# Three gates over the mixers' end, and the mixers' masks and operand products on VectorE, in a one-core hybrid encoder block

## The chip, the cores and the metric

The kernel runs on one core of a Trainium2 chip. The metric is the device time of one execution in microseconds, as the median of three runs. One execution more was taken with the hardware profiler; the profile and the trace are of that execution.

## The reference

One layer of a trunk (256 tokens, width 2048, float32). Every product of a weight matrix with the activations is done in the kernel as a few products of parts (a rounded high part and a low rest), so nearly all of its time is TensorE work on weight tiles.

```python
def hybrid_mixer(u, w_in, ...):
    proj = u @ w_in
    sb, fox, rw, gates = _split(proj, (3 * SB_WIDTH, 3 * FOX_WIDTH + FOX_HEADS, RWKV_IN, N_BRANCHES * D_MODEL))
    y_a = _merge_heads(stick_breaking_attention(...))     # 4 heads x 128, masked strictly below the diagonal
    y_b = _merge_heads(forgetting_attention(...))         # 4 heads x 128
    y_c = rwkv7_time_mix(rw, ...)                         # 16 heads x 64, a recurrence over the 256 tokens
    g_a, g_b, g_c = _split(jax.nn.sigmoid(gates), (D_MODEL,) * 3)
    m = g_a * (y_a @ w_branch_a) + g_b * (y_b @ w_branch_b) + g_c * (y_c @ w_branch_c)
    return m @ w_out

def reference(x, ...):
    u = _rms_norm(x, norm_mix_pre[l])
    x = x + _rms_norm(hybrid_mixer(u, ...), norm_mix_post[l])
    hdn = jnp.square(jax.nn.relu(_rms_norm(x, norm_mlp_pre[l]) @ w_mlp_up[l]))
    x = x + _rms_norm(hdn @ w_mlp_down[l], norm_mlp_post[l])
```

In the stick-breaking attention, `a = where(strict, exp(log_beta + between), 0)`, with the logs masked by the same strict triangle before they are summed.

## The kernel before

**The weight stream.** All weights lie in device memory as one sequence of tiles of 128 x 1024 numbers (512 KB each), `wst`. `wraw` (L159) has SyncE fetch the next tile into one of three `raw` buffers; `wpos` is the place in the sequence and the table `jump` (L153) says where the sequence is left for another place. `wsplit` (L169) makes of each tile a rounded part on ScalarE (L172, `whi`) and the rest on VectorE (L174, `wlo`); three buffers of each. TensorE then multiplies: `unit` (columns, L190, L194, L196) and `tok` (tokens, L234, and L219 for the last tile, which is kept for both token halves). A product on `wlo` has to wait for VectorE's subtraction of that tile, and a tile is prepared one ahead (`AHEAD`).

**The mixers.** The attention and recurrence are one generator, `mixers()`: `sb_mix`, `fox_mix`, `rwkv_lora`, then `rwkv_half` twice (heads 0 to 7 and 8 to 15). It yields between pieces of its work. `tick` (L137), called a few times in each weight tile, lets the generator go on: each tick adds credit, each yield takes off the number that it yields, and a yield of `("stage", cost, hold)` also stops the generator until `hold` worth of ticks have passed (2.0 if none is named). So the yielded numbers and holds set at which place of the weight stream each piece of the mixers stands.

**Order on the engines.** From the first stage on, TensorE's order is the order in which the code is written (a manual schedule of that engine); ScalarE, VectorE and GpSimd are ordered by a scheduler. Each engine then runs its instructions strictly in order.

**The pieces that the change touches.**
- `sb_mix`: the scores `z` (L503, L504 make two logs), masked by the strict triangle `mst` on the diagonal blocks of each head, 8 GpSimd products of 128 x 128 (L507); the masked logs are split (L513, L514) and summed on TensorE (L519 to L522); after the exponential (L534) the same mask again, 8 GpSimd products (L537), ahead of the products with the values (L542, L543).
- `rwkv_half`, `gates`: for each of its four head pairs the scan of log decays (L734), exponentials `ep` and `em` (L737, L738), and the operands of the chunk products: `At` on VectorE (L751, L753) and `Bt` on GpSimd, one product from the normalised key (L750), one from the receptance `r` (L758). TensorE multiplies `At` with `Bt` (L775); the result is masked on VectorE into `SC` (L784). The gates' small projections are L723 (TensorE).
- `rwkv_half`, the triangular inverse: 32 x 32 blocks are transposed into `U` (L814, VectorE), 31 steps of forward substitution (L819, L821) fill `Ti`, and then three more transposes write `TW` (L825) and the blocks of `SC` (L829, twice) that TensorE reads (L834).
- `rwkv_half`, the end: for each two head pairs a group norm (`rsqrt`, L264 to L269), scale, bias, the bonus `bon` and the output gate (L936 to L939), which gives `yc`. TensorE's last instructions of the mixers are L100, L101, L926 and L929.

**The mixers' end.** After the projections of the mixers the stream goes on with gates and branches: `gate` (a projection of `u`, 8 tiles, then a tanh on ScalarE, L1003) and `branch` (a product with the mixers' result, 4 tiles for the third branch). The third branch needs `yc`. So two of its four gates are run first (`thc`, L1033), in which the mixers go on by ticks; what is left of the mixers after that is issued at once (L1034, L1035). `cut` (L1025) splits each finished `yc` into a `pk` tile (L255 on ScalarE, L256 on VectorE). Then come branch 0, branch 1, gate 2, branch 2, gate 3 and branch 3 of the third branch; the evacuations are L1014 and L1015.

```python
    thc = [gate(), gate("BK", 8)]                        # L1033
    while not fin[0]:
        step()
    cut()
```

Names in the trace: `pk` operands are split activations (`u` or `yc`), `g` are the mixers' 128 x 256 tiles, `gn` the group norm's, `gps` are PSUM banks of the weight stream and `mps` those of the mixers.

## Time and profile before

| | us |
|---|---|
| median of 3 runs | 1519.75 |
| lowest, highest | 1519.08, 1521.86 |
| the profiled execution, its own time | 1519.93 |
| span of its trace, first to last instruction | 1518.2 |
| TensorE busy (share of the span) | 1495.3 (98%) |
| VectorE busy | 1208.3 (80%) |
| ScalarE busy | 939.7 (62%) |
| GpSimd busy | 99.6 (7%) |
| mean granted TensorE clock | 0.996 |

In the rows of the profile PE is TensorE's multiplication and PEld its loading of weights, DVE is VectorE, ACT ScalarE, POOL GpSimd, SP SyncE. A row of the timeline reads: start in us from the span's start, duration in us, engine, line, operation, what is written and read, shape, count, and in brackets the engine's idle time before it and what ended it. Successive instructions of one engine may overlap a little, so what an instruction adds to a queue is the distance from its start to the next one's. Equal instructions that follow each other are merged into one row. A few records of matmuls can be missing.

The stages of the span that matter here: `sb_mix` runs from about 65 to 130 us, the gates of the recurrence at 225 to 265 (first half) and 447 to 480 (second half), the two triangular inverses end at 332 and 553, the mixers' end is at 657.6. What follows (the output projection, then the MLP from 845 on) is the same code before and after.

### The profile page before, as it was taken

The numbers are of one execution on the slowest core, as the hardware profiler recorded it, in microseconds if no ns is written. First come the engines' busy times: TensorE is split into PE (matmuls) and PEld (weight loads), VectorE is DVE, ScalarE is ACT, GpSimd is POOL, SyncE is SP. The second block draws the span as 40 slices with busy tenths as digits, with TensorE's granted clock in tenths as the row PEclk, the third lists the DMA queues.
The fourth block names the chain that finished last, engine by engine and source line by source line (L and its number), as shares of the span: only waits on it lengthen the run. The fifth ranks groups of instructions, "written<-read, shape, count | busy, mean of one in ns | idle before, by whom it ended". The sixth has DMA issues, their size and how long they took to land.

```text
span 1518.2 us, 22692 instructions
## 1 busy us (share of the span) xinstructions
PE 1495.3 (98%) x8384; PEld 1254.8 (83%) x8384; DVE 1208.3 (80%) x1663; ACT 939.7 (62%) x1433; POOL 99.6 (7%) x151
## 2 busy tenths in 40 slices
PE   9999999999999999989999999999999999999997
PEld 7888888887787877778888988888888888888886
DVE  7875669985678885565656778999899989999996
ACT  7665677545776445644445766677666666766663
POOL 0031003000002000000000000000000000000000
PEclk9999999999999999999999999999999999999999
DMA  7645454454455464445575758879888888889874
GB/s 266 194 167 181 148 172 156 157 190 144 157 170 181 145 195 147 156 152 194 203 249 189 242 173 263 235 226 275 247 256 265 242 249 245 263 263 259 253 221 151
DMA packets 104687, 312.71 MB, mean 206 GB/s; under 512 B 10240, under 2 KB 12288, under 8 KB 104576
## 3 DMA queue, kind: packets, MB, share of 16 engines
q1 hardware_dynamic: 93968, 279.87, 55.2%
q0 software_dynamic: 8064, 29.36, 10.1%
q10 hardware_dynamic: 2544, 2.03, 0.5%
q8 instruction: 66, 1.08, 0.3%
q14 instruction: 45, 0.37, 0.1%
HBM read 279.77 MB, written 2.10 MB: 186 GB/s over the span
## 4 chain that ended last, share of the span: by engine, by line
PE 86%; DVE 6%; DMA 3%; issue 2%; ACT 2%; DVEq 0%; POOLq 0%; SPq 0%; POOL 0%; ACTq 0%
PE gps L234 25%; PE gps L190 19%; PE gps L194 11%; PE gps L219 7%; PE mps L1363 3%; PE mps L1365 3%; PE mps L1364 3%; PE gps L1363 2%; PE gps L1365 2%; PE gps L1364 2%; DMA raw<-in_wst_dram 2%; DVE wlo L174 2%; PE gps L196 1%; ACT whi L172 1%; DMA raw<-raw 1%
## 5 line engine op out<-in xcount | busy, mean ns | idle before, releaser
L174 DVE TENSOR_TENSOR wlo<-raw,whi 128x1024 fp32r<-128x1024 f32 x576 | 697.7, 1221 | 176.0 <-ACT whi L172 158.5
L172 ACT ACTIVATE whi<-raw 128x1024 fp32r<-128x1024 f32 x576 | 603.9, 1056 | 257.1 <-PE gps L234 91.7
L190 PE MATMUL gps<-pk,whi 128*128 128x512 f32 x1479 | 375.7, 392 | 1.8 <-DVE tmp L1281 1.6
L190 PEld LDWEIGHTS gps<-pk,whi 128*128 128x128 f32 x1479 | 273.9, 188 | 57.7 <-DVE tmp L1281 2.6
L234 PE MATMUL gps<-whi,pk 128*128 128x512 f32 x1004 | 254.6, 392 | 0.0
L194 PEld LDWEIGHTS gps<-pk,wlo 128*128 128x128 f32 x1582 | 215.5, 190 | 15.7 <-DVE wlo L174 0.8
L194 PE MATMUL gps<-pk,wlo 128*128 128x256 f32 x1582 | 221.1, 282 | 0.0
L234 PEld LDWEIGHTS gps<-whi,pk 128*128 128x128 f32 x1004 | 186.4, 188 | 39.7 <-issue 0.8
L234 PE MATMUL gps<-wlo,pk 128*128 128x512 f32 x502 | 137.7, 392 | 1.1 <-DVE wlo L174 1.1
L234 PEld LDWEIGHTS gps<-wlo,pk 128*128 128x128 f32 x502 | 93.2, 188 | 21.9 <-DVE wlo L174 2.0
L1363 PE MATMUL mps<-whi,fm 128*128 128x512 f32 x224 | 88.6, 396 | 0.8 <-ACT whi L172 0.5
L1364 PE MATMUL mps<-whi,fm 128*128 128x512 f32 x224 | 87.7, 392 | 0.0
L1280 ACT ACTIVATE tmp<-gps 128x256 f32<-128x256 f32 x64 | 24.6, 384 | 101.7 <-PE gps L196 99.8
L1365 PE MATMUL mps<-wlo,fm 128*128 128x512 f32 x224 | 87.4, 390 | 0.0
L1343 POOL DMA_DIRECT2D raw<-raw x56 | 48.8, 872 | 573.2 <-DVE raw L1340 279.8
L1340 DVE TENSOR_TENSOR raw<-raw,raw 128x1024 f32<-128x1024 f32 x56 | 68.3, 1220 | 0.8
L219 PE MATMUL gps<-whi,pk 128*128 128x512 f32 x224 | 63.0, 404 | 4.6 <-ACT pk L255 4.6
L1363 PE MATMUL gps<-whi,fm 128*128 128x512 f32 x168 | 65.8, 392 | 0.0
L1365 PE MATMUL gps<-wlo,fm 128*128 128x512 f32 x168 | 65.8, 392 | 0.0
L1364 PE MATMUL gps<-whi,fm 128*128 128x512 f32 x168 | 65.5, 390 | 0.0
L219 PEld LDWEIGHTS gps<-whi,pk 128*128 128x128 f32 x224 | 42.3, 193 | 14.4 <-ACT pk L255 5.0
L1365 PEld LDWEIGHTS mps<-wlo,fm 128*128 128x128 f32 x224 | 42.1, 188 | 9.6 <-DVE wlo L174 0.2
(346 smaller groups left out, 1732.2 us busy)
## 6 DMA issues: line engine op xcount, KB each, us to landing
raw<-in_wst_dram SPq DMA_DIRECT2D x516, 512.0 KB, 4.4
raw<-raw POOLq DMA_DIRECT2D x56, 512.0 KB, 8.2
x<-in_xt_dram SPq DMA_DIRECT2D x8, 256.0 KB, 6.8
x<-in_x_dram SPq DMA_DIRECT2D x8, 256.0 KB, 5.0
raw<-in_wst_dram SPq DMA_DIRECT2D x4, 256.0 KB, 4.8
g<-in_gains_dram SPq DMA_DIRECT2D x4, 256.0 KB, 4.9
pk<-in_gains_dram SPq DMA_DIRECT2D x4, 256.0 KB, 7.4
out_dram<-x SPq DMA_DIRECT2D x4, 256.0 KB, 2.8
```

The source lines that it names most:

```text
L172: A.activation(hi, raw, AF.Copy)
L174: low = lambda: V.tensor_tensor(lo, raw, hi.bitcast(F32), ALU.subtract)
L190: PE.matmul(ps, hi[:, i * 128:i * 128 + 128], pks[i], start=first and i == 0, stop=False)
L194: PE.matmul(ps[:, 0:T], lo[:, i * 128:i * 128 + 128], pks[i][:, 0:T], start=False, stop=False)
L219: PE.matmul(ps[tt], pks[k][:, c:c + 128], w[:, (k - k0) * 512:(k - k0) * 512 + 512], start=k == 0 and part == 0 and w is hl[0], stop=w is ...
L234: PE.matmul(ps[tt], pks[k][:, c:c + 128], w[:, (k - k0) * 512:(k - k0) * 512 + 512], start=k == 0 and part == 0 and w is hl[0], stop=False)
L1280: A.activation(b, ps[:, T:2 * T], AF.Copy)
L1340: V.tensor_tensor(R[d, a], R[d, a], R[d, b], ALU.add)
L1343: G.dma_start(out=R[d, a], in_=R[d, b], accum_op=ALU.add)
L1363: PE.matmul(Q[f], a, w, start=d == d0 and i == 0, stop=False)
L1364: PE.matmul(Q[f], b, w, start=False, stop=False)
L1365: PE.matmul(Q[f], a, wl, start=False, stop=d == dn and i == 1)
```

## The change

Four things are changed.

1. Three gates of the third branch run before its first branch product, not two, and the table `jump` takes the third gate's 8 weight tiles out of their place accordingly. The third gate's tanh lies in two tiles of the tag `BK`, as the second's does.
2. The strict masks of `sb_mix` are done on VectorE, two heads and both diagonal blocks in one instruction of 128 x 2 x 2 x 128 numbers: four VectorE products take the place of sixteen GpSimd ones. The yields there have other costs and shorter holds.
3. The two `Bt` products of each head pair are done on VectorE (16 in all).
4. In `rwkv_half` each transpose of 32 x 32 blocks is cut in two halves with a yield after each; the hold after a head pair's first chunk products is 3.5 for the first pair (it was 2.0), the holds around the last transposes are smaller.

```diff
-    jump = {23: 28, 53: 24, 27: 54, gc + 7: gc + 12, gc + 19: gc + 8, gc + 11: gc + 20}
+    jump = {23: 28, 53: 24, 27: 54, gc + 7: gc + 12, gc + 19: gc + 24, gc + 31: gc + 8,
+            gc + 11: gc + 20, gc + 23: gc + 32}
...
+    def masked(x):
+        d = x.rearrange("p h (b c) -> p h b c", b=3)[:, :, 0:3:2, :]
+        V.tensor_tensor(d, d, C("mst").unsqueeze(1).unsqueeze(1).to_broadcast([128, 2, 2, 128]), ALU.mult)
...
-            for h in (2 * hp, 2 * hp + 1):
-                for c in (0, 256):
-                    G.tensor_tensor(z[:, h, c:c + 128], z[:, h, c:c + 128], C("mst"), ALU.mult)
-            yield ("stage", 1.8, 2 + 6 * hp)
+            masked(z[:, hs])
+            yield ("stage", 2.3, 1)
...
-            for h in (2 * hp, 2 * hp + 1):
-                for c in (0, 256):
-                    G.tensor_tensor(m0[:, h, c:c + 128], m0[:, h, c:c + 128], C("mst"), ALU.mult)
-            yield ("stage", 0.2, 1 + 8 * hp)
+            masked(m0[:, hs])
+            yield ("stage", 0.9, 1 + 2 * hp)
...
-            G.tensor_tensor(Bt[p][:, :, 0:64], kn4, ep[:, :, 0:64], ALU.mult)
+            V.tensor_tensor(Bt[p][:, :, 0:64], kn4, ep[:, :, 0:64], ALU.mult)
...
-            G.tensor_tensor(Bt[p][:, :, 64:128], r.rearrange("p (c t) -> p c t", c=4), ep[:, :, 1:65], ALU.mult)
+            V.tensor_tensor(Bt[p][:, :, 64:128], r.rearrange("p (c t) -> p c t", c=4), ep[:, :, 1:65], ALU.mult)
...
-            yield ("stage", 1.6)
+            yield ("stage", 1.6, 3.5 if i == 0 else 2.0)
...
-            V.transpose(out=U[br], in_=SC[br, :, 32 * b:32 * b + 32].rearrange("s l t -> s t l"))
-            yield 1.3
+            for c in (slice(0, 16), slice(16, 32)):
+                V.transpose(out=U[br, c], in_=SC[br, :, 32 * b:32 * b + 32][:, :, c].rearrange("s l t -> s t l"))
+                yield 0.65
...
-        V.transpose(out=TW[0:32].rearrange("t l i -> t i l"), in_=Ti[0:32].rearrange("l t i -> l i t"))
-        yield 1.3
+        for c in (slice(0, 16), slice(16, 32)):
+            V.transpose(out=TW[0:32, :, c].rearrange("t l i -> t i l"), in_=Ti[0:32, :, c].rearrange("l t i -> l i t"))
+            yield 0.65
...
-            V.transpose(out=SC[br, :, 32 * b:32 * b + 32].rearrange("i l t -> i t l"), in_=Ti[br])
-            yield ("stage", 1.3, 1 + 3 * b)
+            for c in (slice(0, 16), slice(16, 32)):
+                V.transpose(out=SC[br, :, 32 * b:32 * b + 32][:, :, c].rearrange("i l t -> i t l"), in_=Ti[br, c])
+                yield ("stage", 0.65, 0.5 + 3 * b * (c.start > 0))
...
-    thc = [gate(), gate("BK", 8)]
+    thc = [gate(), gate("BK", 8), gate("BK", 8)]
```

Four lines are added on the whole, so a line of the kernel after stands one to four lines below its fellow before (L174 is L175, L219 is L220, L234 is L235, L255 is L256, L750 is L751, L929 is L933, L1003 is L1007).

**How the instructions move: TensorE at the mixers' end.** Before, after the mixers' last TensorE instructions, the stream goes on with the first tile of branch 0, whose activation operands (`pk_5947`, `pk_5950`) are split `yc`:

```order
L929 MATMUL mps_6517<-zz,gup_6480 128x256
L929 MATMUL mps_6518<-zz,gup_6480 128x256
L234 MATMUL gps_6546<-whi_6496,pk_5947 128x512 x2
L234 MATMUL gps_6547<-whi_6496,pk_5947 128x512 x2
L234 MATMUL gps_6546<-whi_6496,pk_5950 128x512 x2
L234 MATMUL gps_6547<-whi_6496,pk_5950 128x512 x2
L234 MATMUL gps_6546<-wlo_6497,pk_5947 128x512
```

Now the same two instructions stand in the second tile of the third gate, whose operands (`pk_267` to `pk_279`) are split `u`:

```order
L933 MATMUL mps_6553<-zz,gup_6500 128x256
L933 MATMUL mps_6554<-zz,gup_6500 128x256
L235 MATMUL gps_6514<-wlo_6519,pk_267 128x512
L235 MATMUL gps_6515<-wlo_6519,pk_267 128x512
L235 MATMUL gps_6514<-whi_6536,pk_268 128x512 x2
L235 MATMUL gps_6515<-whi_6536,pk_268 128x512 x2
L235 MATMUL gps_6514<-whi_6536,pk_269 128x512 x2
```

After these rows come the rest of that tile and six more gate tiles, and only then the four tiles of branch 0; before, branch 0 came at once. In both, the first three tiles of branch 0 read `yc` 0 to 5 and the last one (L219, now L220) reads `yc` 6 and 7.

**ScalarE at the same place.** Before, the splits of the last two `yc` (`pk_6540`, `pk_6543`) come behind the group norm's tables and three weight tiles, and the next gate's tanh is far behind them:

```order
L172 ACTIVATE whi_6568<-raw_6566 128x1024
L265 ACT_TABLE_LOAD
L265 ACTIVATE gn_6485<-gn_6485 128x512
L172 ACTIVATE whi_6586<-raw_6584 128x1024
L172 ACTIVATE whi_6604<-raw_6602 128x1024
L172 ACTIVATE whi_6628<-raw_6626 128x1024
L937 ACTIVATE g_1119_5867<-g_1119_5867,par 128x256
L937 ACTIVATE g_1120_5868<-g_1120_5868,par 128x256
L255 ACTIVATE pk_6540<-g_1119_5867 128x256
L255 ACTIVATE pk_6543<-g_1120_5868 128x256
```

Now they stand ahead of the third gate's tanh (`th_6684`, `th_6692`):

```order
L173 ACTIVATE whi_6620<-raw_6618 128x1024
L173 ACTIVATE whi_6638<-raw_6636 128x1024
L941 ACTIVATE g_1122_5887<-g_1122_5887,par 128x256
L941 ACTIVATE g_1123_5888<-g_1123_5888,par 128x256
L173 ACTIVATE whi_6656<-raw_6654 128x1024
L256 ACTIVATE pk_6588<-g_1122_5887 128x256
L256 ACTIVATE pk_6615<-g_1123_5888 128x256
L173 ACTIVATE whi_6674<-raw_6672 128x1024
L173 ACTIVATE whi_6698<-raw_6696 128x1024
L1007 ACTIVATE th_6684<-gps_6514 128x512
L1007 ACTIVATE th_6692<-gps_6515 128x512
```

What moved is the third gate's evacuation, from behind two branches to just behind the last split.

**VectorE in the gates of the first half.** The piece is where the second head pair's operands are made. Before (`wlo` rows are the weight tiles 73 and 74 of the kernel's whole ones):

```order
L174 TENSOR_TENSOR wlo_2405<-raw_2402,whi_2404 128x1024
L640 TENSOR_SCALAR g_449_2352<-tmp_2354,omu,zp_2355 128x256
L762 TENSOR_TENSOR hl_2376<-g_442_2319,hl_2376 128x256
L745 TENSOR_SCALAR kkr_2417<-g_331_1830,par,b_376_2045 128x256
L174 TENSOR_TENSOR wlo_2448<-raw_2445,whi_2447 128x1024
L743 TENSOR_TENSOR g_466_2414<-g_466_2414,g_331_1830 128x256
L746 TENSOR_SCALAR tha_2381<-tha_2381,em_2382 128x256
L753 TENSOR_TENSOR At_2420<-g_466_2414,em_2382 128x4x64
L751 TENSOR_SCALAR At_2420<-kkr_2417,tha_2381 128x4x64
```

Now, the same two tiles:

```order
L175 TENSOR_TENSOR wlo_2393<-raw_2390,whi_2392 128x1024
L763 TENSOR_TENSOR hl_2364<-g_442_2307,hl_2364 128x256
L746 TENSOR_SCALAR kkr_2405<-g_331_1818,par,b_376_2033 128x256
L744 TENSOR_TENSOR g_466_2402<-g_466_2402,g_331_1818 128x256
L747 TENSOR_SCALAR tha_2369<-tha_2369,em_2370 128x256
L751 TENSOR_TENSOR Bt_2409<-kkr_2405,ep_2371 128x4x64
L752 TENSOR_SCALAR At_2408<-kkr_2405,tha_2369 128x4x64
L754 TENSOR_TENSOR At_2408<-g_466_2402,em_2370 128x4x64
L639 TENSOR_TENSOR tmp_2425<-gps_2349,tmp_2424 128x256
L175 TENSOR_TENSOR wlo_2436<-raw_2433,whi_2435 128x1024
```

Eight operations stand between the two low parts where three stood: the second pair's products, `Bt` among them (L751), have come ahead of the low part `wlo_2436`. Ahead of `wlo_2393`, between it and the low part before it, stand nine operations where six stood, two of them the first pair's `Bt`.

**VectorE at the end of the first triangular inverse.** Before, one low part lies between each two transposes or behind them:

```order
L174 TENSOR_TENSOR wlo_3442<-raw_3439,whi_3441 128x1024
L640 TENSOR_SCALAR g_669_3399<-tmp_3401,omu,zp_3402 128x256
L825 STREAM_TRANSPOSE TW_3453<-Ti_2995 32x32x32
L174 TENSOR_TENSOR wlo_3480<-raw_3477,whi_3479 128x1024
L829 STREAM_TRANSPOSE SC_2258<-Ti_2995 32x32x32
L638 TENSOR_TENSOR tmp_3467<-gps_3408,tmp_3466 128x256
L829 STREAM_TRANSPOSE SC_2258<-Ti_2995 32x32x32
L640 TENSOR_SCALAR g_681_3465<-tmp_3467,omu,zp_3468 128x256
L174 TENSOR_TENSOR wlo_3499<-raw_3496,whi_3498 128x1024
```

Now the halves, of which two stand further ahead, within the substitution:

```order
L175 TENSOR_TENSOR wlo_3509<-raw_3506,whi_3508 128x1024
L823 TENSOR_TENSOR Ti_2995<-Ti_2995,tp_2996 64x31
L828 STREAM_TRANSPOSE TW_3475<-Ti_2995 32x16x32 x2
L833 STREAM_TRANSPOSE SC_2246<-Ti_2995 32x16x32
L175 TENSOR_TENSOR wlo_3528<-raw_3525,whi_3527 128x1024
L833 STREAM_TRANSPOSE SC_2246<-Ti_2995 32x16x32
L175 TENSOR_TENSOR wlo_3547<-raw_3544,whi_3546 128x1024
```

The longest row of transposes between two low parts is now three halves (`TW` twice, `SC` once), where two whole ones and an evacuation stood.

## The prediction

> **What bounds the kernel now.** The sections of busy time come first, then the waits of TensorE, longest in total first (who waits for whom; total, count, longest, in us):
>
> ```profile
> PE 1495.3 (98%) x8384; PEld 1254.8 (83%) x8384; DVE 1208.3 (80%) x1663; ACT 939.7 (62%) x1433; POOL 99.6 (7%) x151
> PE gps L219 <- ACT pk L255: 4.6, 1, 4.6
> PE gps L190 <- DVE tmp L1281: 1.6, 2, 0.8
> PE gps L234 <- DVE wlo L174: 1.1, 2, 0.9
> PE gps L219 <- DVE wlo L174: 1.0, 2, 0.6
> PE mps L723 <- DVE SC L784: 0.9, 1, 0.9
> ```
>
> TensorE is the bound: the change takes no product from it, so a gain can only be a wait that goes, and a loss only a new one. One wait is far longer than the rest. L1281 belongs to the MLP, which stays as it is. The timeline of the long wait, branch 0's last tile for the split of `yc` 6 and 7:
>
> ```profile
> 643.90 0.70 PE L929 MATMUL mps<-zz,gup 32*128 32x256 f32 x4
> 650.10 1.98 PE L234 MATMUL gps<-whi,pk 128*128 128x512 f32 x8
> 656.68 0.74 DVE L939 TENSOR_TENSOR g<-mps,g 128x256 f32<-128x256 f32 x2
> 657.13 0.75 ACT L255 ACTIVATE pk<-g 128x256 fp32r<-128x256 f32 x2 [1.38 <-DVE g L939]
> 657.60 2.11 PE L219 MATMUL gps<-whi,pk 128*128 128x512 f32 x4 [4.61 <-ACT pk L255]
> 662.66 1.98 PE L234 MATMUL gps<-whi,pk 128*128 128x512 f32 x8
> 665.38 0.84 PE L234 MATMUL gps<-whi,pk 128*128 128x512 f32 x3
> ```
>
> From TensorE's last mixer instruction to the split runs a chain of some 13.1 us (644.5 to 657.6; group norm, scale, bonus, gate), and only three tiles of branch 0 lie over it. The twelve matmuls of the tile behind the wait take from 657.60 to 662.66, 5.06 us; the twelve of the next take from 662.66 to 665.38, 2.72. The windows (span, then busy time of PE, PEld, DVE, ACT, POOL, the granted clock, DMA share, GB/s) say why:
>
> ```profile
> 240.00:252.00 12.00, 11.12 (x80) 9.20 (x79) 11.52 (x22) 8.10 (x17) 1.42 (x5) 1.00 0.62 206
> 652.00:664.00 12.00, 7.39 (x23) 5.59 (x22) 8.64 (x16) 3.96 (x6) 0.00 (x0) 0.72 0.39 132
> 664.00:676.00 12.00, 12.00 (x54) 9.95 (x53) 8.50 (x10) 4.70 (x5) 0.00 (x0) 1.00 0.51 175
> ```
>
> The clock was 0.72 in the window behind the long wait and 1.00 in the one after. So the long wait cost twice: 4.61 of idle time and 5.06 − 2.72 = 2.34 of slow clock. The short wait of L723 (first of these rows, 0.88 of idle time) left the clock at 1.00.
>
> [...]
>
> **The third gate (part 1).** The same chain now has more over it. The mixers' last instructions stand in the third gate's second tile, and behind them come the rest of that tile and six more, then the three tiles of branch 0 that need only `yc` 0 to 5: nine whole tiles of 2.72 are 24.5 us, for a chain of 13.1. ScalarE gets more in between, but the gate's tanh stands behind the splits. About 11 us are spare, so the wait goes, and the slow clock with it: **6.95**. No tile is added; the three gates' tiles are fetched in another order in one queue, whose transfers are as many as before. If that cover failed, it would cost the whole 6.95 again.
>
> **The masks (part 2).** Two instructions ahead of the sums on TensorE and two behind them replace sixteen on GpSimd. No row shows the new form; the nearest on VectorE is L784, also a product with a mask broadcast, 512 numbers a partition, and the nearest for the old work is GpSimd's own:
>
> ```profile
> L784 DVE TENSOR_TENSOR SC<-mps,con 128x512 f32<-128x512 f32 x11 | 7.1, 682 | 0.1
> L537 POOL TENSOR_TENSOR sbm<-sbm,con 128x128 f32<-128x128 f32 x8 | 4.4, 590 | 9.4 <-ACT sbm L534 9.4
> 92.58 11.19 POOL L507 TENSOR_TENSOR sbt<-sbt,con 128x128 f32<-128x128 f32 x8 [0.79 <-DVE sbt L504]
> 104.69 0.96 DVE L514 TENSOR_TENSOR zs<-sbt,zs 128x768 fp32r<-128x768 f32 x1 [1.24 <-ACT zs L513]
> 109.44 0.40 PE L519 MATMUL mps<-zs,cr 128*128 128x512 f32 x1
> ```
>
> I take 0.62 for a mask (0.68 less the overlap with the next); the far end is four of GpSimd's, 4 × 0.59 = 2.36. Two masks are so 1.2 us of VectorE where GpSimd had 11.19, to 103.77, and held up the second rest (L514). TensorE's sums stand two tiles, 5.44, earlier in the stream: the second group is due at 109.44 − 5.44 = 104.0. Walking VectorE's new order from the first log on, I get that rest at about 103.4. That is near, with low parts of weight tiles (1.2 each) queued between: I take **0.3 lost**, between 0 and 1.2, one low part. The two masks behind the sums have tile after tile over them and cost nothing; at 2.36 each they would cost 3.5 more.
>
> **The operand products (part 3).** VectorE about the second pair of the first half, and TensorE's use of the low part written at 238.07:
>
> ```profile
> 235.32 1.19 DVE L174 TENSOR_TENSOR wlo<-raw,whi 128x1024 fp32r<-128x1024 f32 x1
> 236.44 0.47 DVE L640 SCALAR_TENSOR_TENSOR g<-tmp,omu,zp 128x256 f32<-128x256 f32 x1
> 236.84 0.91 DVE L762 TENSOR_TENSOR hl<-g,hl 128x256 fp32r<-128x256 f32 x1
> 237.67 0.47 DVE L745 SCALAR_TENSOR_TENSOR kkr<-g,par,b 128x256 f32<-128x256 f32 x1
> 238.07 1.21 DVE L174 TENSOR_TENSOR wlo<-raw,whi 128x1024 fp32r<-128x1024 f32 x1
> 239.20 0.91 DVE L743 TENSOR_TENSOR g<-g,g 128x256 f32<-128x256 f32 x1
> 239.33 1.22 PE L194 MATMUL gps<-pk,wlo 128*128 128x256 f32 x8
> 240.03 0.41 DVE L746 SCALAR_TENSOR_TENSOR tha<-tha,em 128x256 f32<-128x256 f32 x1
> 240.37 0.41 DVE L753 TENSOR_TENSOR At<-g,em 128x256 f32<-128x256 f32 x1
> 240.70 0.41 DVE L751 SCALAR_TENSOR_TENSOR At<-kkr,tha 128x256 f32<-128x256 f32 x1
> L758 POOL TENSOR_TENSOR Bt<-g,ep 128x256 f32<-128x256 f32 x8 | 8.7, 1087 | 0.0
> ```
>
> Operations of one kind step by 0.34 (L753 to L751) or by 0.83 (L762, L743, 0.91 long); the long ones fall where GpSimd makes its products (L758, 1.09 each). So each product on GpSimd cost VectorE about what VectorE now needs to make it, and what counts is the order. Ahead of the low part in question stand now, between the two low parts before it, nine operations (seven of 0.34, and so on, 3.4 in all), and then eight: L762's and the six other plain ones at 0.34, L745's at 0.40, 2.8. From the same start the tile of 235.32 starts at 235.4, and the next at 235.4 + 1.13 + 2.8 = 239.3, and ends at 240.5, for a use at 239.33. Its end was just in time before; now TensorE waits **1.2**. Ends: 0, if VectorE runs ahead by then, and 1.2 + 3 × 0.5 = 2.7, if the three `Bt` products go at the slow step. L723, one tile's unit later in the stream now, finds its `SC` done: the **0.88** goes. In the second half the same crowding adds about 1 us, and the work stands 0.9 later: its waits stay as they are, between 0.7 better and 1.5 worse.
>
> **The transposes (part 4).** At the end of the first inverse a whole transpose stands ahead of a low part that TensorE wants:
>
> ```profile
> L829 DVE STREAM_TRANSPOSE SC<-Ti 32x1024 f32<-32x1024 f32 x4 | 8.1, 2016 | 0.1
> L825 DVE STREAM_TRANSPOSE TW<-Ti 32x1024 f32<-32x1024 f32 x2 | 4.3, 2126 | 0.0
> 329.68 2.06 DVE L829 STREAM_TRANSPOSE SC<-Ti 32x1024 f32<-32x1024 f32 x1
> 333.44 1.20 PE L234 MATMUL gps<-wlo,pk 128*128 128x512 f32 x4 [0.91 <-DVE wlo L174]
> 550.94 0.72 PE L219 MATMUL gps<-wlo,pk 128*128 128x512 f32 x2 [0.56 <-DVE wlo L174]
> ```
>
> Half a transpose is half the elements, about 1.03. The longest row between two low parts is three halves, 3.1, where it was two whole ones, 4.1, and other work: 1 us less against waits of 0.91 and 0.56. Both go: **1.47**. If a half cost as much as a whole, both would stay and grow by 1.
>
> **The sum.** 6.95 + 0.88 + 1.47 − 1.2 − 0.3 = 7.8. The profiled execution took 1519.93, so 1512.1; the median of the three runs, 1519.75, is 0.18 below it.
>
> **The rivals.** *All small waits go too:* VectorE is ahead at both places where I put a new wait, and the rest of the waits for low parts in the recurrence (of 1.1 + 1.0 in the list, 0.6 beside the two named) go as well: 6.95 + 0.88 + 1.47 + 0.6 = 9.9, **1510.0**. For it: no product of GpSimd slows VectorE any more; against: the low part of 239.33 has no slack.
>
> *VectorE gives much of it back:* the products go at the slow step even with GpSimd still (2.7 lost in the first half), the sum waits the full 1.2, the transposes' and L723's waits are only replaced: 6.95 − 2.7 − 1.2 = 3.1, **1516.9**. For it: 11.52 of 12.00 busy in the window from 240. Against it: the step of 0.34.
> [...]
>
> *The end stays uncovered:* something holds the chain until the branch is reached, such as the third gate's tanh tiles, which share a tag with the operand products. The 6.95 stays, and the rest nets nothing: **1519.9**. Against it: the splits stand ahead of that tanh.
>
> *Slower:* the broadcast forms run on VectorE at GpSimd's pace. Two masks of 2.36 come 2 × 1.74 later, of which the 0.6 to spare takes up a little, so the sum waits 2.9; the masks behind, their cover used up, lose 3.5; the products at the slow step lose 2.7 and 1.5 in the two halves; the small waits stay. 10.6 against the 6.95: **1523.6**. It decides from the point where the new waits pass 6.95. Against it: L784, a broadcast too, has 1.3 ns a number, and L753, with the same 4 × 64 view, 0.41 us.
>
> **How the numbers follow.** Forecast 0.72, all small waits 0.07, much given back 0.13, uncovered 0.03, slower 0.05. From no change a measurement of this kernel can tell 0.2%, 3.0 us, so faster ends at 1516.7. The third rival straddles that bound, so half of it is the same: faster 0.72 + 0.07 + 0.07 = 0.86, same 0.06 + 0.03 = 0.09, slower 0.05. The likeliest case alone runs from 1510.6 (both new waits 0) to about 1515: all three unknown waits at their far ends would add 1.5 + 0.9 + 1.5 = 3.9, and I take three quarters of that. The range goes to 1509.0 below and 1516.4 above, and leaves out the slower half of the third rival and the last two.
>
> **What would show it.** In the profile after: no wait of TensorE for a split at L220, and a clock of 1.00 all through the mixers' end (part 1). GpSimd's L507 and L537 gone, masks near 0.65, and a wait of at most 1.2 at the first sums (part 2). Short operations in steps of 0.34 between 228 and 252, one wait of about 1.2 for a low part there, and none at L724 (part 3). Half transposes of about 1.05, and no waits for low parts near 332 and 551 (part 4). The prediction is wrong if the split's wait is still there, if a mask takes over 2, or if the waits for low parts in the mixers sum to over 4.

## The result, and the profile after

| | before | after |
|---|---|---|
| median, us (20 runs each) | 1518.38 | 1513.05 |
| lowest, highest | 1516.52, 1521.86 | 1511.39, 1518.17 |
| the profiled execution, its own time | 1519.93 | 1518.09 |

The ratio of after to before is 0.9966, with a 95% interval of 0.9959 to 0.9974: 5.2 us less, where 7.8 were forecast from the first three of the runs of before. The profiled execution of after is one of the slowest of its 20, so the two profiles are compared place by place, not by their spans.

The waits of TensorE in the profile after (who waits for whom; total, count, longest):

```profile
PE gps L191 <- ACT whi L173: 2.7, 2, 2.5
PE gps L235 <- DVE wlo L175: 1.9, 1, 1.9
...
PE gps L195 <- DVE wlo L175: 1.1, 1, 1.1
...
PE mps L845 <- ACT TW L841: 0.7, 4, 0.3
```

The wait for the split (4.6), that of `SC` (0.9) and those for low parts near 333 and 551 are gone. There are three new ones in the mixers: 1.1 in the first half's gates, 1.9 in the second's, 0.7 in the first triangular inverse (L845). The 2.7 of L191 is nearly all one wait in the MLP, which has the same code before and after:

```profile
1218.35 3.36 PE L191 MATMUL gps<-pk,whi 128*128 128x512 f32 x7 [2.52 <-ACT whi L173]
```

With the slow clock behind it (0.50 from 1218.38 to 1221.79 us, seven matmuls in 3.36 us), it is probably the main reason why this execution lies high. No other profile of this study had it, and why it came was not found.

**The mixers' end.** The timeline after, on TensorE and ScalarE:

```profile
652.21 0.70 PE L933 MATMUL mps<-zz,gup 32*128 32x256 f32 x4
662.99 0.75 ACT L256 ACTIVATE pk<-g 128x256 fp32r<-128x256 f32 x2 [0.42 <-DVE g L943]
667.02 1.07 PE L220 MATMUL gps<-whi,pk 128*128 128x512 f32 x4
677.90 1.07 PE L220 MATMUL gps<-whi,pk 128*128 128x512 f32 x4
```

The split ends at 663.7, while the third gate still runs (its last tile is the L220 of 667.02); branch 0's last tile, which needs it, starts at 677.90 with no wait, 14 us later. The windows there (span, busy time of PE, PEld, DVE, ACT, POOL, the granted clock, DMA share, GB/s):

```profile
652.00:664.00 12.00, 12.00 (x55) 9.56 (x54) 9.13 (x15) 9.25 (x13) 0.00 (x0) 1.00 0.63 196
664.00:676.00 12.00, 12.00 (x55) 9.93 (x54) 6.09 (x8) 6.27 (x7) 0.00 (x0) 1.00 0.62 205
```

TensorE is busy all the time at a clock of 1.00, where before it was busy for 7.39 of 12 us at 0.72.

**The first half's gates.** VectorE and TensorE after, at the place whose low part was in question:

```profile
234.92 1.20 DVE L175 TENSOR_TENSOR wlo<-raw,whi 128x1024 fp32r<-128x1024 f32 x1
236.04 0.42 DVE L763 TENSOR_TENSOR hl<-g,hl 128x256 fp32r<-128x256 f32 x1
...
237.44 0.42 DVE L751 TENSOR_TENSOR Bt<-kkr,ep 128x256 f32<-128x256 f32 x1
...
238.78 1.22 DVE L175 TENSOR_TENSOR wlo<-raw,whi 128x1024 fp32r<-128x1024 f32 x1
240.05 1.21 PE L195 MATMUL gps<-pk,wlo 128*128 128x256 f32 x8 [1.05 <-DVE wlo L175]
250.30 0.98 PE L724 MATMUL mps<-xs,lors 64*128 64x256 f32 x12
```

Eight operations fill 236.04 to 238.78, 2.74 us (2.8 were forecast); none is 0.91 long any more (they are 0.42 and one 0.48), now that GpSimd makes no product. TensorE waits 1.05, on the one low part in question. L724, which waited 0.88 before, does not.

**The second half's gates.** The same view at 461 to 470 us:

```profile
461.99 0.68 DVE L1018 SCALAR_TENSOR_TENSOR th<-th,gps 128x512 f32<-128x512 f32 x1
...
463.93 0.68 DVE L1019 TENSOR_TENSOR m<-m,th 128x512 f32<-128x512 f32 x1
464.53 0.68 DVE L1018 SCALAR_TENSOR_TENSOR th<-th,gps 128x512 f32<-128x512 f32 x1
465.13 1.21 DVE L175 TENSOR_TENSOR wlo<-raw,whi 128x1024 fp32r<-128x1024 f32 x1
466.40 1.21 PE L235 MATMUL gps<-wlo,pk 128*128 128x512 f32 x4 [1.86 <-DVE wlo L175]
467.43 3.57 PE L235 MATMUL gps<-whi,pk 128*128 128x512 f32 x8
```

Ahead of the low part stand eleven operations, among them the second pair's products and three of the four evacuations of a branch (L1018, L1019). The eight matmuls behind the wait take 3.57 us, not the usual 1.98.

**The first inverse.** Its two products are L838 and L845; between them ScalarE copies the first one's result (L841):

```profile
343.72 1.06 ACT L173 ACTIVATE whi<-raw 128x1024 fp32r<-128x1024 f32 x1 [2.66 <-DMA raw<-in_wst_dram]
344.81 1.57 ACT L841 ACTIVATE TW<-mps 32x256 f32<-32x256 f32 x4
345.23 0.24 PE L845 MATMUL mps<-SC,TW 32*32 32x32 f32 x2 [0.26 <-ACT TW L841]
...
346.43 0.70 PE L845 MATMUL mps<-SC,TW 32*32 32x32 f32 x58 [0.16 <-ACT TW L841]
```

The copies are queued behind a weight tile's split, which waits for that tile's transfer, and L845 waits for one copy after another. The clock about this place and about the second half's wait:

```profile
344.00:348.00 4.00, 3.27 (x73) 2.26 (x72) 1.73 (x2) 3.84 (x8) 0.00 (x0) 1.00 0.63 215
348.00:352.00 4.00, 4.00 (x23) 2.81 (x22) 0.72 (x1) 2.61 (x6) 0.00 (x0) 0.58 0.56 202
464.00:468.00 4.00, 2.13 (x9) 1.45 (x8) 4.00 (x6) 0.73 (x1) 0.00 (x0) 0.93 0.15 44
468.00:472.00 4.00, 4.00 (x14) 2.88 (x14) 3.90 (x7) 1.47 (x2) 0.11 (x1) 0.64 0.80 259
```

In this execution the clock fell at both: (1 − 0.58) × 4 = 1.7 us lost at the inverse, (0.07 + 0.36) × 4 = 1.7 at the second half (where the waits for low parts came to 0.69 before). So two places that the prediction costed at a gain or at nothing cost 0.7 + 1.7 and (1.86 − 0.69) + 1.7.

The new instructions themselves, grouped by line (total, then mean ns):

```profile
L484 DVE TENSOR_TENSOR sbt<-sbt,con 128x512 f32<-128x512 f32 x2 | 1.4, 677 | 0.0
L833 DVE STREAM_TRANSPOSE SC<-Ti 32x512 f32<-32x512 f32 x8 | 8.7, 1093 | 0.1
L828 DVE STREAM_TRANSPOSE TW<-Ti 32x512 f32<-32x512 f32 x4 | 4.4, 1138 | 0.1
```

A mask takes 0.68 us as its nearest row said, a half transpose 1.09 to 1.14 against 1.03 assumed. TensorE's first sums wait for nothing.

### The profile page after: what moved, and what is told of

It reads as the page before. It is cut to its first block, busy times and chain, and to the rows that moved or that the text cites. A ratio compares the mean times of both kernels' runs of the same rounds, so it can differ in the third digit from the quotient of the medians.

```text
span 1516.3 us, 22684 instructions
## 1 busy us (share of the span) xinstructions
PE 1496.9 (99%) x8384; PEld 1257.4 (83%) x8384; DVE 1209.1 (80%) x1693; ACT 939.7 (62%) x1433; POOL 69.2 (5%) x119
## 4 chain that ended last, share of the span: by engine, by line
PE 89%; DVE 6%; ACT 2%; DMA 2%; issue 2%; DVEq 0%; POOLq 0%; POOL 0%; SPq 0%; ACTq 0%
PE gps L235 26%; PE gps L191 20%; PE gps L195 11%; PE gps L220 7%; PE mps L1367 3%; PE mps L1368 3%; PE mps L1369 3%; PE gps L1369 2%; PE gps L1367 2%; PE gps L1368 2%; DVE wlo L175 2%; DMA raw<-in_wst_dram 1%; PE gps L197 1%; ACT whi L173 1%; PE mps L776 1%
## 5 line engine op out<-in xcount | busy, mean ns | idle before, releaser
L175 DVE TENSOR_TENSOR wlo<-raw,whi 128x1024 fp32r<-128x1024 f32 x576 | 697.0, 1220 | 161.4 <-ACT whi L173 148.7
L191 PE MATMUL gps<-pk,whi 128*128 128x512 f32 x1479 | 377.1, 393 | 2.7 <-ACT whi L173 2.7
L191 PEld LDWEIGHTS gps<-pk,whi 128*128 128x128 f32 x1479 | 274.8, 189 | 58.2 <-ACT whi L173 3.8
L235 PE MATMUL gps<-whi,pk 128*128 128x512 f32 x1004 | 254.6, 394 | 0.0
L235 PEld LDWEIGHTS gps<-whi,pk 128*128 128x128 f32 x1004 | 187.6, 189 | 40.4 <-issue 0.8
L235 PE MATMUL gps<-wlo,pk 128*128 128x512 f32 x502 | 139.5, 394 | 1.9 <-DVE wlo L175 1.9
L235 PEld LDWEIGHTS gps<-wlo,pk 128*128 128x128 f32 x502 | 92.9, 188 | 22.3 <-DVE wlo L175 2.3
L220 PE MATMUL gps<-whi,pk 128*128 128x512 f32 x224 | 61.5, 397 | 0.0
L1367 PEld LDWEIGHTS mps<-whi,fm 128*128 128x128 f32 x224 | 42.4, 189 | 9.0 <-ACT whi L173 2.9
```

What stands on the lines that cost most here:

```text
L175: low = lambda: V.tensor_tensor(lo, raw, hi.bitcast(F32), ALU.subtract)
L191: PE.matmul(ps, hi[:, i * 128:i * 128 + 128], pks[i], start=first and i == 0, stop=False)
L220: PE.matmul(ps[tt], pks[k][:, c:c + 128], w[:, (k - k0) * 512:(k - k0) * 512 + 512], start=k == 0 and part == 0 and w is hl[0], stop=w is ...
L235: PE.matmul(ps[tt], pks[k][:, c:c + 128], w[:, (k - k0) * 512:(k - k0) * 512 + 512], start=k == 0 and part == 0 and w is hl[0], stop=False)
L1367: PE.matmul(Q[f], a, w, start=d == d0 and i == 0, stop=False)
```

## The experiments

Each kernel was timed in five rounds beside the kernel before; ratios are to it, and a ratio of 0.001 is 1.5 us. A ratio can differ from the quotient of the two medians by up to 0.0004. The intervals are some ±0.0012 wide, so most of these kernels cannot be told from each other by their times alone, and the profile is asked what moved. A profile shows one execution.

**The end alone.** The kernel before with `jump` and `thc` of the change:

```diff
-    thc = [gate(), gate("BK", 8)]
+    thc = [gate(), gate("BK", 8), gate("BK", 8)]
```

> The kernel before with three gates over the mixers' end and nothing else. Theory: the end is worth what the prediction gave it, 4.61 us of waiting and about 2.3 of slow clock, 6.9 us less than the kernel before (ratio 0.9955), more than the whole change brings (5.3), since the other parts lose on balance. Rival: the end brings less than 5.3 (ratio over 0.9965), and the shortfall lies there.

Measured: 0.9952 (0.9940 to 0.9964), median 1511.59. The end is worth what it was put at (7.3 us by the ratio, 6.6 by the medians). Its interval overlaps with the whole change's, but all five of its times (1510.38 to 1511.92) lie below 18 of the changed kernel's 20: the change as a whole brings less than this part alone, and the rest of it loses on balance.

**All but the end.** The changed kernel with two gates (and `jump` as before):

```diff
-    thc = [gate(), gate("BK", 8), gate("BK", 8)]
+    thc = [gate(), gate("BK", 8)]
```

> The changed kernel with two gates over the mixers' end, as before; masks, operand products and transposes as changed. Theory: the other three parts lose on balance: the wait for the split is back (4.6 us and a slow clock), the time is 1 to 3 us above the kernel before (ratio 1.001 to 1.002). Rival: the other parts gain the 0.9 us of the prediction (0.88 + 1.47 - 1.2 - 0.3) or more, ratio 0.9994 or less.

Measured: 1.0022 (1.0014 to 1.0031), median 1521.70. The other three parts lose on balance without the gate too, a little more than the theory said. How much they lose beside it can't be read off here, since the end came out in another way. TensorE's timeline of this run:

```profile
646.50 0.50 PE L100 MATMUL mps<-hl,cr 128*128 128x512 f32 x1 [3.16 <-ACT hl L922]
...
650.08 3.78 PE L234 MATMUL gps<-whi,pk 128*128 128x512 f32 x8
...
661.34 0.50 PE L219 MATMUL gps<-whi,pk 128*128 128x512 f32 x1 [0.55 <-ACT pk L255]
```

The mixers' pieces stand a tile later than before, so more of them is left when the two gates are done, and TensorE waits inside them, with nothing else ahead of it.

**The load behind the last transpose.** The second half's `lora` is loaded into the inverse's buffer, so its issue, on ScalarE, waits for the last transpose. The timeline of the changed kernel there:

```profile
336.68 1.09 DVE L833 STREAM_TRANSPOSE SC<-Ti 32x512 f32<-32x512 f32 x1
337.81 0.33 ACTq L675 DMA_DIRECT2D lor<-in_lora_dram  x1
338.26 1.06 ACT L173 ACTIVATE whi<-raw 128x1024 fp32r<-128x1024 f32 x1 [3.03 <-DVE SC L833]
```

ScalarE stands idle for 3.03 us, with a weight tile's split queued behind the issue. Moved to GpSimd's queue:

```diff
-            nc.scalar.dma_start(out=lraw, in_=lora[:, 512 * hf:512 * hf + 512])
+            (nc.gpsimd if hf else nc.scalar).dma_start(out=lraw, in_=lora[:, 512 * hf:512 * hf + 512])
```

> The changed kernel, with the second half's load of lora issued on GpSimd's queue rather than ScalarE's. Theory: this load, which waits for the last transpose, holds ScalarE for 3 us and so delays weight tiles, and the four waits of L845 near 345 us (0.7 us) and the clock of 0.58 behind them come from it. They go, and the time is 2.5 to 3.3 us below the changed kernel's, some 8 below the kernel before (ratio 0.9945 to 0.995). Rival: the late weight tiles come from busy transfers, not from ScalarE; the waits stay and the ratio is the changed kernel's, 0.9966.

Measured: 0.9958 (0.9946 to 0.9969), median 1511.83. The waits of L845 shrank to 0.2, as the theory had it, but the gain is about half of what was expected and lies inside the intervals. Two later runs with the same edit had 0.3 and 0.8 there: the load is at most a part of the cause.

**The second half's products.** The changed kernel with them on GpSimd:

```diff
-            V.tensor_tensor(Bt[p][:, :, 0:64], kn4, ep[:, :, 0:64], ALU.mult)
+            (G if hf else V).tensor_tensor(Bt[p][:, :, 0:64], kn4, ep[:, :, 0:64], ALU.mult)
...
-            V.tensor_tensor(Bt[p][:, :, 64:128], r.rearrange("p (c t) -> p c t", c=4), ep[:, :, 1:65], ALU.mult)
+            (G if hf else V).tensor_tensor(Bt[p][:, :, 64:128], r.rearrange("p (c t) -> p c t", c=4), ep[:, :, 1:65], ALU.mult)
```

> The changed kernel, with the Bt products of the second half back on GpSimd; those of the first half stay on VectorE. Theory: the products ahead of the low part that TensorE awaits at 466.4 us (1.86 us) are what made it late; without them it comes at least 1 us earlier, the wait is under 0.8 and the clock stays at 1.00 there: 2 to 3.5 us below the changed kernel's, ratio about 0.9945 to 0.9955. Rival: GpSimd's products slow VectorE by as much as they take off its queue, or the branch's evacuations are what crowds it: the wait stays between 1.3 and 2.4, ratio 0.996 to 0.997.

Measured: 0.9953 (0.9941 to 0.9965), median 1511.63. The time is as the theory said, the wait is not: 1.16, between the two.

```profile
467.39 1.19 PE L235 MATMUL gps<-wlo,pk 128*128 128x512 f32 x4 [1.16 <-DVE wlo L175]
```

**All products on GpSimd**, in the same two lines with `G` for both halves.

> The changed kernel, with the Bt products of both halves back on GpSimd. Theory: the low part that TensorE awaits for 1.1 us near 239.7 us comes in time again, L724 has no wait (its hold is still 3.5), and the second half's wait is 1.2 as with its products alone on GpSimd: about 1 us below that run, ratio 0.9940 to 0.9950. Rival: GpSimd's products slow VectorE's short operations to 0.91 us again and take back what they free: a wait of 0.8 or more near 240 us, ratio 0.995 to 0.996.

Measured: 0.9949 (0.9937 to 0.9962), median 1510.41. Both halves of the theory about the first half hold: no wait between 228 and 252 us. (Two operations beside GpSimd's first pair of products step by 0.84 and 0.83 again, L754 at 232.02 us and L752 at 232.86, but ahead of another low part.) The second half's wait is 1.86 again, though its products are not on VectorE: the scheduler put all four evacuations ahead of the low part, 2.4 us:

```profile
462.33 1.27 DVE L1018 SCALAR_TENSOR_TENSOR th<-th,gps 128x512 f32<-128x512 f32 x2
463.52 1.28 DVE L1019 TENSOR_TENSOR m<-m,th 128x512 f32<-128x512 f32 x2
464.73 1.21 DVE L175 TENSOR_TENSOR wlo<-raw,whi 128x1024 fp32r<-128x1024 f32 x1
```

So that low part is this late without the products in VectorE's queue. They still cost VectorE something there, since L754 and L752, ahead of these rows, step by 0.82 and 0.84 beside them; but the evacuations are the larger part.

**Whole transposes.** The changed kernel with the transposes and their holds as before:

```diff
-            for c in (slice(0, 16), slice(16, 32)):
-                V.transpose(out=SC[br, :, 32 * b:32 * b + 32][:, :, c].rearrange("i l t -> i t l"), in_=Ti[br, c])
-                yield ("stage", 0.65, 0.5 + 3 * b * (c.start > 0))
+            V.transpose(out=SC[br, :, 32 * b:32 * b + 32].rearrange("i l t -> i t l"), in_=Ti[br])
+            yield ("stage", 1.3, 1 + 3 * b)
```

and `U` and `TW` likewise.

> The changed kernel, with the transposes whole and the holds around them as before. Theory: the halves gained 1.5 us for the low parts and their later place lost about as much through the load of lora behind the last one: here waits of 0.9 and 0.6 for low parts near 335 and 553 us are back, those of L845 are gone; the ratio lies within 0.0007 of the changed kernel's 0.9966. Rival: the halves are a gain of 1.5 us as predicted, and the waits of L845 have another cause and stay: ratio 0.9976 or more.

Measured: 0.9962 (0.9949 to 0.9974), median 1512.10. No wait at L845, as the theory had it. But the low parts' waits came back as one of 0.49 only, near 560 us: a tile later in the stream, whole transposes cost little. So here the cut gains 0.5 and loses 0.7 and, in the profile after, 1.7 of slow clock. The inverse's second product (L842 in this kernel) starts just as the last copy ends:

```profile
343.68 1.58 ACT L838 ACTIVATE TW<-mps 32x256 f32<-32x256 f32 x4
345.29 0.75 PE L842 MATMUL mps<-SC,TW 32*32 32x32 f32 x64
```

**The masks on GpSimd**, with their yields as before:

```diff
-            masked(z[:, hs])
-            yield ("stage", 2.3, 1)
+            for h in (2 * hp, 2 * hp + 1):
+                for c in (0, 256):
+                    G.tensor_tensor(z[:, h, c:c + 128], z[:, h, c:c + 128], C("mst"), ALU.mult)
+            yield ("stage", 1.8, 2 + 6 * hp)
```

and `m0` likewise.

> The changed kernel, with the masks of the first attention on GpSimd with their holds as before. Theory: the masks are hidden in both places, TensorE waits for none of them, and the ratio is the changed kernel's 0.9966 within 0.0007. Rival: their place, or GpSimd's slowing of VectorE in 92 to 104 us, is worth over 1.5 us either way (under 0.9955 or over 0.9977).

Measured: 0.9958 (0.9945 to 0.9972), median 1510.98. TensorE waits for no mask in either kernel. The ratio lies 0.0008 under the changed kernel's, a hair more than the theory allowed and well within the interval: the masks can't be told from no change.

**Three causes taken away**: the load on GpSimd's queue, all products on GpSimd, and

```diff
-            yield ("stage", 1.6, 3.5 if i == 0 else 2.0)
+            yield ("stage", 1.6, 3.5 if i == 0 and hf == 0 else 2.0)
```

> The changed kernel with three edits: the second half's load of lora on GpSimd's queue, all Bt products back on GpSimd, and the longer hold of 3.5 only in the first half. Theory: the three causes found add up: no wait of over 0.3 at L845, none over 0.3 in 228 to 252 us, and 0.7 in all for low parts near 460 us as in the kernel before; about 3 us below the changed kernel and 1 to 2 below the kernel with the gate alone (ratio 0.9952): 0.9935 to 0.9945. Rival: the small waits move on to the next tiles whatever is done, and the ratio is 0.995 or more.

Measured: 0.9959 (0.9947 to 0.9972), median 1511.98: the rival's number. L845 waits 0.3, no low part near 240 us is late, but that of the second half is, by 1.87. The hold was put back in the half where it was not at fault. What is left is the first half's longer hold, which moves what comes behind it, the second half's gates included, one tile down the stream. The runs bear this out: with the masks' yields as before (the run above) the second half's wait is still 1.87, and with 2.0 in both halves (the next run) the waits there are before's, 0.49 at L220 and 0.22 at L235 where 0.46 at L219 and 0.23 at L234 stood.

**The third gate and the cut transposes alone**, on the kernel before, with the diffs shown above.

> The kernel before with the third gate and the cut transposes, nothing else. Theory: the halves alone gain what the prediction gave them, 1.5 to 1.8 us below the kernel with the gate alone (ratio 0.9952), since the waits of 0.9 and 0.5 near 332 and 551 us go and, the pieces standing a tile earlier than in the changed kernel, the load of lora holds ScalarE by less: no wait of over 0.3 at L845. Ratio 0.9935 to 0.9945. Rival: the last transposes come later by their holds alone, the load behind them holds ScalarE as in the changed kernel, waits of 0.5 or more at L845 come, and the ratio is 0.995 or more.

Measured: 0.9960 (0.9946 to 0.9973), median 1511.59, the rival's side: no gain over the gate alone. The wait near 332 us is gone. That near 551 is not: all four halves that end the second inverse stand ahead of one low part here, 4.3 us, and 0.59 stands where the gate alone has 0.54. And L845 waits 0.9, without the change's hold and without a long stall behind the load (ScalarE's split behind it waits 1.05).

```profile
342.92 0.24 PE L845 MATMUL mps<-SC,TW 32*32 32x32 f32 x2 [0.38 <-ACT TW L841]
556.72 1.20 PE L235 MATMUL gps<-wlo,pk 128*128 128x512 f32 x4 [0.59 <-DVE wlo L175]
```

So the cut itself, with its holds, brings L845's wait. Its yields come in smaller pieces, and between the inverse's two products they leave 14 matmuls of weight tiles where 18 stood with whole transposes: 4 × 0.226 = 0.9 us less (2.72 us are 12 matmuls).

**The second half's place.** The changed kernel with its second half's gates a tile earlier:

```diff
-        yield ("stage", 0.8, 3)
+        yield ("stage", 0.8, 3 - hf)
```

> The changed kernel, with one hold (after the second half's lora is split) 2 for 3, so that the second half's gates stand a tile earlier, where the kernel before has them; all products stay on VectorE. Theory: place and products each add to the queue ahead of the low part; with the products there the four evacuations of branch 0 still lie ahead of the same low part, and a wait of 1 to 2 us stays: ratio 0.996 to 0.9968. Rival: only the place counts, the wait falls to the kernel before's 0.7 in all, and the ratio is 0.9945 to 0.9955.

Measured: 0.9964 (0.9952 to 0.9977), median 1512.49. The wait halves, and stays near 0.9.

```profile
464.18 1.20 PE L235 MATMUL gps<-wlo,pk 128*128 128x512 f32 x4 [0.89 <-DVE wlo L175]
```

**Place and products**: the run with three causes taken away, with this edit too.

> The run with the three edits (load on GpSimd's queue, Bt products on GpSimd, longer hold in the first half only), and that hold 2 for 3 as well. Theory: the second pair's operations come ahead of branch 0's evacuations again, so the wait of 1.9 us falls below 0.8; 1 to 1.5 us below the run without it (0.9959 +- 0.0012): 0.9945 to 0.9953. Rival: the wait only moves to another low part and stays over 1.3; the ratio is unchanged.

Measured: 0.9940 (0.9928 to 0.9953), median 1509.39. Together (and with the load moved) they do it, with a little more gained than the theory said:

```profile
465.00 0.74 PE L235 MATMUL gps<-wlo,pk 128*128 128x512 f32 x2 [0.32 <-DVE wlo L175]
```

**Room between the inverse's products**, on that run:

```diff
         for g in range(4):
             A.activation(TW[32:64, g:32:4, :], ps[32 * g:32 * g + 32, 0:256].rearrange("p (a b) -> p a b", a=8), AF.Copy)
-        yield ("stage", 0.2, 2)
+        yield ("stage", 0.2, 2.5)
```

> The fastest run so far (ratio 0.9940: three gates, cut transposes, load on GpSimd's queue, Bt products on GpSimd, earlier place of the second half), with a hold of 2.5 for 2 between the inverse's two products, which puts six matmuls of the weight stream (1.4 us) more between them. Theory: the waits of L845 (0.8 us there, and none where the transposes are whole) come from the cut transposes' yields, which leave 14 matmuls of weight tiles between the two products where 18 stood, 0.9 us less; with 20 they go, and the time is 0.5 to 1.5 us lower, 0.9932 to 0.9938. Rival: the copies on ScalarE are late because their weight tile comes late, whatever stands between; they stay late by the same, L845 still waits 0.3 us or more, and the ratio is unchanged.

Measured: 0.9931 (0.9918 to 0.9945), median 1507.56. L845 has no wait:

```profile
344.75 1.58 ACT L841 ACTIVATE TW<-mps 32x256 f32<-32x256 f32 x4
346.40 0.75 PE L845 MATMUL mps<-SC,TW 32*32 32x32 f32 x64
```

The copies run at the same time as in the changed kernel (344.81 there); the product now stands behind them. The intervals of this run and the one before overlap, so the gain in time is not shown by itself. By its median this is the fastest kernel of the study, about 5 us below the changed one.

## Why the prediction was right, and where it was short

The direction, the range (1509.0 to 1516.4) and the bulk of the gain hold; the gain was forecast at 7.8 and measured at 5.2. The time itself, 1513.05 against 1512.1, came nearer than the gain, and that is luck: the forecast was counted from the first three runs of before, whose median lies 1.4 above that of all 20. Term by term, from the profile after:

| term of the sum | forecast | profile after |
|---|---|---|
| the end (wait and slow clock) | −6.95 | wait gone, clock 1.00; alone 0.9952, 7.3 us |
| L723 | −0.88 | gone |
| low part of the first half | +1.2 | +1.05 |
| first sums | +0.3 | no wait |
| transposes | −1.47 | both waits gone (whole ones leave 0.49 here); L845 +0.7, and a slow clock of 1.7 |
| second half's low parts | 0 | 0.69 became 1.86, +1.2, and a slow clock of 1.7 |

Without the slow clocks that is −6.95 − 0.88 + 1.05 − 1.47 + 0.7 + 1.2 = −6.4; with both, −3.0. The measured −5.2 lies between.

**What held.** The third gate's cover and the double price of the long wait (4.61 and 2.34 of slow clock); that a product on GpSimd costs VectorE about what it would cost there (before, operations beside GpSimd's products stepped by 0.83 and not 0.34, some 0.5 us more each; on VectorE a `Bt` product steps by 0.33), so that the order counts (with all products on GpSimd again the first half's wait is gone, by another order, and the steps of 0.83 are back); the wait of 1.2, from the steps of eight operations; the mask's price.

**What failed, first: "Both go: 1.47."** Both did, but for the larger part not by the halves: whole transposes at the changed kernel's place leave a wait of 0.49 alone, so some 1.0 of the 1.47 came with the later place, which the step did not count. At before's place the halves took one wait of two away. And the step counted only what waits for VectorE behind a transpose, and not what the smaller yields do to the pieces behind it. These set where the next TensorE instructions of the inverse stand in the stream, and they brought its second product 0.9 us closer to the first, with copies on ScalarE in between that already ended just in time. The cut alone lost what it gained (0.9960 beside 0.9952 for the gate alone, with overlapping intervals and the same median; of the waits, one of 0.9 went and 0.9 at L845 came); whole transposes took L845's wait away, and so did six matmuls of room. That the load of `lora` behind the last transpose was the cause was my first theory, and it fell: with the load moved away the wait was still 0.8 in one run.

**What failed, second: "its waits stay as they are"**, for the second half. The bound of 1.5 us worse took in the 1.2, the value taken did not. The step counted the products that were added, and credited 0.9 us for the later place. The place is a whole tile, 2.72, later, and the step left out what stands there: three evacuations of a branch come ahead of the same low part, 1.8 us of VectorE (all four, 2.4 us, in the run with the products on GpSimd). Products alone off VectorE left 1.16 or 1.86, the place alone 0.89, both together, with the load moved as well, 0.32. The hold that took L723's 0.88 away, in the first half, is what moved the second half there.

**Rivals.** "VectorE gives much of it back" was the nearest in its place, not in its mechanism: no short operation ran at the slow step, and the sums did not wait. A rival in which the holds move later pieces into other work would have been the right one, and was not on the list.

**Open.** How often the clock was slow in the executions that were not profiled, and so how the 1.2 us between the measured gain and the sum of −6.4 divide. An estimate from the numbers of the last section fits: if the edges of windows of 3.41 us fall anywhere alike, which no run here shows, a wait of 1.86 lies whole in one of them in (3.41 − 1.86) / 3.41 = 0.45 of all executions (two of seven profiles had the slow clock there), and three of eight profiles with 0.5 us or more of waiting at L845 had it at the inverse; at 1.7 us each that is 0.8 + 0.6 = 1.4. But stages with the same code differ by as much between profiles: TensorE's waits for `tmp` in the MLP came to 1.6 us in the profile before and to none in that after. The cause of the MLP's wait of 2.52 us is open.

## What to carry to other kernels

Where the order of work is set by yields and holds, a change of one of them is a change of the place of everything behind it: list, for each later piece, what it now stands next to, on each engine, and not only at the place that was meant. A wait that was removed by moving something down the stream has to be looked for again where that something's successors meet the next crowd. And parts of a change are worth timing one by one: here one of four carried all the gain, and others gave part of it back in places that the diff doesn't name.

## What was not expected of the hardware

The same wait does not always slow the clock. Of seven profiles with a wait of about 1.86 us at the second half's low part, two had a slow clock behind it (from 468 to 472 us 0.64 in the changed kernel and 0.57 in that with its masks on GpSimd); five had 1.00. The timeline of the kernel with its load on GpSimd's queue:

```profile
464.10 1.20 PE L235 MATMUL gps<-wlo,pk 128*128 128x512 f32 x4 [1.87 <-DVE wlo L175]
465.13 1.98 PE L235 MATMUL gps<-whi,pk 128*128 128x512 f32 x8
```

The eight matmuls behind the wait take 1.98 us here; behind the same wait in the changed kernel they took 3.57.

The windows can be cut at the edges of a slow stretch. Three rows of the changed kernel, then two of that with whole transposes, which had the same wait (its edges counted back from the half clock in which its trace ends):

```profile
464.03:467.44 3.41, 1.54 (x8) 0.95 (x7) 3.41 (x5) 0.70 (x1) 0.00 (x0) 1.00 0.02 8
467.44:470.86 3.42, 3.42 (x10) 2.65 (x9) 3.34 (x7) 1.47 (x2) 0.11 (x1) 0.50 0.88 285
470.86:474.27 3.41, 3.41 (x30) 2.75 (x29) 2.27 (x3) 1.66 (x2) 0.00 (x0) 1.00 0.77 233
460.59:464.00 3.41, 1.69 (x8) 1.07 (x6) 3.41 (x7) 1.34 (x2) 0.00 (x0) 1.00 0.06 23
464.00:467.41 3.41, 3.27 (x14) 2.73 (x15) 3.41 (x6) 0.56 (x2) 0.11 (x1) 1.00 0.56 185
```

The clock is 0.50 for a window of 3.41 us, or for two of them: 655.52 to 662.35 us in the kernel before. There TensorE worked again from 657.60 on, so 4.75 us ran at half the clock, 2.4 lost, which is the 2.34 of the long wait. In the changed kernel such windows start at 347.98, 467.44 and 1218.38 us, 35 and then 220 times 3.413 apart, and the half clock in which its trace ends starts at 1511.92, 86 times 3.413 later: in this execution they lie on a fixed grid. There the wait lies whole in one window, with TensorE busy for 1.54 us in it, and the next has the clock of 0.50. With whole transposes the wait runs from 462.28 to 464.14 us, so that the edge at 464.00 cuts it; the emptier window still has 1.69 us of work, and no slow window follows. That the place of the edges decides would fit these two profiles; for the other five it is not shown.

At the inverse less waiting was enough in three profiles: with 0.7 us at L845 in the changed kernel, 0.8 with its masks on GpSimd and 0.9 with the third gate and the cut transposes alone, a window of 4 us there had a clock of 0.58, 0.57 and 0.71. Five others with 0.5 to 0.8 us had 1.00. In the changed kernel TensorE was busy for 2.68 of the 3.41 us ahead of the slow window (344.57 to 347.98), part of that on 64 matmuls of 32x32. What tells the three from the five no run here shows.

The 20 runs of the changed kernel fit with slow windows in some of them, without showing it: the mean clock was 0.995 in those of 1516.50 and 1518.09 us, and 0.998 in five of 1511.48 to 1512.74; but it was 0.996 in one of 1512.84 and 0.999 in one of 1514.46. So waits near 1.9 us are worth removing here for their slow clock as well, which two of seven profiles show, and perhaps for the spread. The waits of 0.91 near 333 us in the kernel before, of 1.05 near 240 us in the changed one, and at the second half's low part of 0.89 (gates a tile earlier) and 1.16 (products on GpSimd) left the clock at 1.00 in the windows of 4 us about them.
